# Opening of a transformer block on one core: the order of two accumulators' products, of one tile's squaring, and of the second half's transposes

## The chip, the cores and the metric

The kernel runs on one core of a Trainium2 chip. The metric is the device time of one execution in microseconds. Three executions of the kernel before took 1181.06, 1181.30 and 1181.48 us; the median is 1181.3.

The core has five engines with one instruction queue each. TensorE (PE in the profile, with its weight loads listed apart as PEld) multiplies matrices into PSUM, VectorE (DVE) and ScalarE (ACT) do elementwise work, GpSimd (POOL) does small elementwise work here, and SyncE (SP) issues most of the loads. Each queue is worked through in order; engines wait for one another by semaphores.

## The reference

One layer of a hybrid encoder: an RMSNorm with adaptive scale and shift, a combined projection, two head groups side by side (a state-space group and a chunked attention group), an output projection, a gated feed-forward part with a short convolution, and a final RMSNorm. Sequence 1024, width 1024, float32. Cut to what the change touches:

```python
c_act = jax.nn.silu(c)
mod = (c_act @ w_ada[l] + b_ada[l])[:, None, :]
sh_m, sc_m, g_m, sh_f, sc_f, g_f = jnp.split(mod, 6, axis=-1)
h = rmsnorm(x, norm_mix_w[l]) * (1 + sc_m) + sh_m
z, xbc, dt_raw, q, k, v = jnp.split(h @ w_in[l], IN_SPLITS, axis=-1)
y_ssd = ssd_mixer(z, xbc, dt_raw, ...)
y_att = chunk_attention(q, k, v, rel_bias[l])
x = x + g_m * (jnp.concatenate([y_ssd, y_att], axis=-1) @ w_out[l])
h = rmsnorm(x, norm_ffn_w[l]) * (1 + sc_f) + sh_f
x = x + g_f * conv_ffn(h, w_up[l], ffn_conv_w[l], w_down[l])
return rmsnorm(x, final_norm_w)
```

The opening of the kernel computes h, and from it q and k of the first two head pairs and v of the same pairs.

## The kernel before

**Numbers in two parts.** Every float32 operand of a large product is split into a high part and a low part (float32r), and a product is three matmuls, high x high, high x low and low x high (`mm3`, lines 83 to 86). Splitting costs one conversion for the high part and one subtraction for the low part (`split`, lines 88 to 94).

**Tiles of the opening.** The 1024 tokens are eight x tiles of 128 tokens (`xts`, tiles 0 to 7); tiles 0 to 3 are the first half (hh = 0), tiles 4 to 7 the second (hh = 1). The 1024 features are eight feature blocks of 128 (kt = 0 to 7). An x tile is loaded (`x_load`, L324), squared and summed along its features (`x_square`: ScalarE's Square with an accumulator, L287, and a small step that adds epsilon, L331; or one VectorE reduction, L333), turned into a reciprocal root on GpSimd (`x_rstd`, L339) and scaled in place (`x_scale`, L345 on ScalarE, L347 on VectorE). The tables `XL`, `XS` and `XM` (L37 to L39) say for tiles 4 to 7 at which feature block of the first half each is loaded, squared and scaled.

**An h block** (`h_block`, L295 to L307) is one feature block of one half, transposed: four TensorE transposes of 128x128, one for each x tile, into a PSUM bank (`tp`; there are two such banks), then the adaptive scale and shift, which also splits. In the first half ScalarE makes the high part (hH, L303) and a float32 copy (hf, L304); in the second ScalarE makes hf alone and VectorE casts it to hH (L306). VectorE's subtraction makes the low part (hL, L307). There are two hf buffers.

**What is multiplied.** For each half there are four accumulators of 128x512 (`accs`, acc in the profile: q and k of pair 0, q and k of pair 1) and two banks for v (`vps`, 128x256 twice in each). A feature block adds 12 matmuls of 128x512 (`first_qk`) and 12 of 128x256 (`first_v`). For each feature block of the first half the kernel also reduces two rows of w_ada on VectorE (`mod_col`, L146) to the scale and shift (amix, L435; bmix, L212), loads the weights (L440) and splits them: wsh on ScalarE (L442), wsl on VectorE (L444).

**Evacuation.** v's banks go out through ScalarE and VectorE (`evac_v`, L413). A q or k accumulator goes out as a high part by ScalarE (L243, L250) and a low part by VectorE (L244, L253), followed by transfers between partitions on SP's queue (L238). The first half's fourth accumulator is copied whole to `k1` by ScalarE (L485), because its place is still taken by an x tile, and is split at the end of the second half.

**What sets the order.** The program is written as one stream; a scheduler that simulates time puts each engine's instructions in order, and each engine then works strictly through its queue. Where `T.on` (or `V.on`, `A.on`) is true, instructions of that engine keep the order in which they are written; `tc.issue_after(i)` forces an instruction behind another. In the first half, feature blocks 0 to 5 are multiplied as they come, and blocks 6 and 7 are the tail, in written order: v's products of both blocks, v's evacuation, then each accumulator's products of both blocks and its evacuation, with the second half's h blocks 0 and 1 behind the second accumulator. In the second half, blocks 0 to 3 are multiplied as they come and blocks 4 to 7 are the tail, an accumulator at a time; h blocks 2 to 7 are written one in each step kt = 2 to 7.

The opening starts the kernel and ends near 97 us, where attention has begun. Nothing behind it is changed.

Of the kernel before, what the change touches and what calls it, by code (L numbers as in the profile page):

```python
# [10 lines left out]
F32 = mybir.dt.float32  # L11
# [5 lines left out]
P = 128  # L17
D = 1024
S = 1024
KT = D // P  # L20
NT = S // P
# [12 lines left out]
GP = {1: {0: ((2, 0, BOTH), (2, 1, BOTH)), 2: ((2, 2, BOTH),)},  # L34
      2: {0: ((3, 0, BOTH), (3, 1, H0)), 2: ((3, 2, H0),)},
      3: {0: ((3, 1, H1),), 1: ((3, 2, H1),)}}
XL = (3, 5, 7, 7)  # L37
XS = (4, 6, 7, 7)
XM = (7, 7, 7, 7)  # L39
WARM = (8, 22)  # L40
KH = NF // 2

# [30 lines left out]
def tile_block(ctx: ExitStack, tc: tile.TileContext, x, ccol, pk, w_ada, w_first, w_ft, w_z,  # L73
# [221 lines left out]
    def h_block(hh, kt, js=(0, 1, 2, 3), tps=None):  # L295
        tps = h_tp(hh, kt) if tps is None else tps
        tmp = s0.tile([P, 512], F32, tag="hf", bufs=2, name="hf")
        b = slice(js[0], js[-1] + 1)
        hi, lo = (t[:, b] for t in ht(hh, kt))
        tps, tmp = c4(tps)[:, b], c4(tmp)[:, b]  # L300
        ab = dict(scale=amix[:, kt:kt + 1], bias=bmix[:, kt:kt + 1])
        if hh == 0:
            A.activation(hi, tps, AF.Identity, **ab)  # L303
        i = A.activation(tmp, tps, AF.Identity, **ab)  # L304
        if hh:
            V.tensor_copy(hi, tmp)  # L306
        return i, V.tensor_tensor(lo, tmp, f32(hi), ALU.subtract)  # L307
# [9 lines left out]
    xts = []  # L317
# [7 lines left out]

    def x_square(st, eng):
        ms = stat()
        junk = s0.tile([P, D], F32, tag="junk", name="junk") if eng is A else xts[NT - 2]
        if eng is A:
            norm_to(xts[st], junk, ms)  # L330
            A.activation(ms, ms, AF.Identity, bias=mhalf[:, 7:8])  # L331
        else:
            V.tensor_tensor_reduce(out=junk, in0=xts[st], in1=xts[st], scale=1.0 / D, scalar=EPS,  # L333
                                   op0=ALU.mult, op1=ALU.add, accum_out=ms)
        return ms

    def x_rstd(ms):
        r = stat()
        G.tensor_tensor(r, ms, mhalf[:, 0:1], ALU.pow)  # L339
        return r  # L340
# [25 lines left out]
    for j in range(2):  # L366
        k = slice(4 * j, 4 * j + 4)
# [23 lines left out]
    def first_qk(acc, n, hh, kts, js=slice(0, 4)):  # L391
        w = slice(n * P, (n + 1) * P)
        for kt in kts:
            mm3(c4(acc)[:, js], wsh[:, kt, w], ws_lo(kt)[:, w], *(t[:, js] for t in ht(hh, kt)),
                kt == 0 and js.start == 0, kt == KT - 1, hh == 0)
# [19 lines left out]
    xr = {}  # L415
    for hh in range(2):
        accs = [(ps0, ps0b)[n // 2].tile([P, 512], F32, tag="acc0", bufs=2, name="acc0") for n in range(4)]
        vps = [psv.tile([P, 2, 256], F32, tag=t, bufs=1, name="vps") for t in ("acc", "pv")]
        split_at = KT - (2, 4)[hh]
        evj = []  # L420

        def ev_half():
            if not evj:
                t = s0.tile([P, D], F32R, tag="junk", name="evl")
                evj.extend((t[:, 512:1024], t[:, 0:512]))
            return evj.pop()

        evs.append(ev_half)
        tail = range(split_at, KT)
        for kt in range(KT):  # L430
            if hh == 0:
                at = last_lo.ins if kt == 1 else bm.ins if kt else None
                mod_col(SC_M + kt, wu.tile([P, 1024], F32, tag="wh", name="adat"), at)
                mod_col(SH_M + kt, adw[:, kt % 2, :], at)
                V.scalar_tensor_tensor(amix[:, kt:kt + 1], modc[:, SC_M + kt:SC_M + kt + 1],  # L435
                                       pkt[:, NMIX + kt:NMIX + kt + 1], am1[:, kt:kt + 1],
                                       op0=ALU.mult, op1=ALU.add)
                bm = mod_shift(bmix, SH_M, kt)
                t = raw_tile(768)
                nc.sync.dma_start(t, w_first[kt])  # L440
                with tc.issue_after(bm.ins) if not kt else ExitStack():
                    (A.activation(wsh[:, kt, :], t, AF.Copy) if kt else V.tensor_copy(wsh[:, kt, :], t))  # L442
                with tc.issue_after(bm.ins):
                    V.tensor_tensor(ws_lo(kt), t, f32(wsh[:, kt, :]), ALU.subtract)  # L444
                for st in range(4, NT):
                    if XL[st - 4] == kt:
                        V.tensor_copy(xts[st][:, 0:1], amix[:, min(kt, 6):min(kt, 6) + 1])
                        x_load(st)
            if hh == 0 or kt > 1:
                hb = i, last_lo = h_block(hh, kt, tps=None if hh or not kt else tps)  # L450
            if hh == 0 and kt == 0:
                x_scale(3, r3, A, rest)
                V.on = A.on = T.on = False
            if hh == 0 and kt < KT - 1:
                tps = h_tp(0, kt + 1)
            if hh == 0:
                for st in range(4, NT):
                    if XS[st - 4] == kt:
                        with tc.issue_after(i.ins):
                            xr[st] = x_rstd(x_square(st, A))  # L460
                    if XM[st - 4] == kt:
                        e = A if st < 6 else V
                        with tc.issue_after((i if e is A else last_lo).ins):
                            x_scale(st, xr[st], e)
            if hh == 1 and kt == 3:
                wpin = hb
            if kt < split_at:
                for n in range(4):
                    first_qk(accs[n], n, hh, (kt,))
                first_v(vps, hh, (kt,))  # L470
        T.on, T.last = True, None
        if hh == 0:
            first_v(vps, 0, tail)
            evac_v(vps, 0)
            for n in range(4):
                first_qk(accs[n], n, 0, tail)
                if n == 1:
                    for kt in range(2):
                        T.on = False
                        h_block(1, kt)  # L480
                        T.on = True
                if n < 3:
                    evac_qkv(n // 2, n % 2, 0, accs[n], None, None)
            k1 = s0.tile([P, 512], F32, name="k1")
            A.activation(k1, accs[3], AF.Copy)  # L485
        else:
            for n in range(4):
                first_qk(accs[n], n, 1, tail)
                if n == 3:
                    es_0a.close()  # L490
                    ps1 = es_p1.enter_context(tc.tile_pool(name="ps1", bufs=1, space=PSUM,
                                                           reuse_waits="tile"))
                    s00 = scores(0, 0)
                    first_v(vps, 1, tail)
                evac_qkv(n // 2, n % 2, 1, accs[n], None, None)
            evac_v(vps, 1)
            evac_qkv(1, 1, 0, k1, None, None)
        T.on = False
# [1263 lines left out]
```

## Time and profile before

| | |
|---|---|
| median of three runs (lowest to highest) | 1181.3 us (1181.06 to 1181.48) |
| the profiled execution | 1181.23 us, of which the span from first to last instruction is 1179.5 us |
| granted TensorE clock, mean | 0.993 |
| TensorE busy from 0 to 24 us | 18.70 us |
| TensorE busy from 24 to 97 us | 70.95 of 73.00 us |
| TensorE busy from 97 us to the end | 1064.15 of 1082.5 us |

Rows of the timeline give the start in us from the span's start, the length in us, the engine, the line, the operation and its tiles as out<-in, the partitions and elements, and how many like instructions are merged (xN); in brackets stands the idle time before it and the instruction that ended it. Rows of waits give the total in us, how often, and the longest. Rows by stage give the stretch, its length, the busy time and the number of instructions of an engine, then the granted TensorE clock (1.00 is full), the share of the DMA engines' time and GB/s. A matmul's end is modelled: consecutive starts tell the pace better than lengths. Tile names are without buffer numbers: tp is a transposed block's bank, qk an x tile or, later, a q or k tile in the same place, wsh and wsl the weights' parts, raws and adat buffers of loads.

### The profile page before, as it was taken

The numbers are of one execution on the slowest core, as the hardware profiler recorded it, in microseconds if no ns is written. First come the engines' busy times: TensorE is split into PE (matmuls) and PEld (weight loads), VectorE is DVE, ScalarE is ACT, GpSimd is POOL, SyncE is SP. The second block draws the span as 40 slices with busy tenths as digits, with TensorE's granted clock in tenths as the row PEclk, the third lists the DMA queues.
The fourth block names the chain that finished last, engine by engine and source line by source line (L and its number), as shares of the span: only waits on it lengthen the run. The fifth ranks groups of instructions, "written<-read, shape, count | busy, mean of one in ns | idle before, by whom it ended". The sixth has DMA issues, their size and how long they took to land.

```text
span 1179.5 us, 15776 instructions
## 1 busy us (share of the span) xinstructions
PE 1153.8 (98%) x5831; PEld 975.9 (83%) x5831; DVE 906.5 (77%) x1350; ACT 586.8 (50%) x981; POOL 155.8 (13%) x179
## 2 busy tenths in 40 slices
PE   8999999999999999999999999999999999999996
PEld 7878888788889888887788888888888888888885
DVE  6736455588895678558999988898888869666986
ACT  5726555664345575487444453434433445433454
POOL 2003333340000165200000000000000000000622
PEclk8999999999999999999999999999999999999998
DMA  8735323155577532141233222332233378633444
GB/s 327 275 97 142 82 81 85 39 179 174 185 254 284 193 112 87 63 152 36 90 116 134 94 82 96 131 124 73 98 107 116 117 271 300 249 118 124 161 134 152
DMA packets 63741, 169.15 MB, mean 143 GB/s; under 512 B 6880, under 2 KB 7344, under 8 KB 62256
## 3 DMA queue, kind: packets, MB, share of 16 engines
q1 hardware_dynamic: 56320, 143.11, 36.6%
q10 hardware_dynamic: 7344, 25.04, 5.4%
q8 instruction: 46, 0.75, 0.3%
q14 instruction: 31, 0.25, 0.1%
HBM read 125.87 MB, written 32.81 MB: 135 GB/s over the span
## 4 chain that ended last, share of the span: by engine, by line
PE 78%; DVE 11%; ACT 4%; issue 3%; DMA 3%; POOL 1%; SPq 0%; POOLq 0%; ACTq 0%; DVEq 0%
PE wops L874 6%; PE dn L86 5%; PE dn L85 5%; PE dn L84 5%; PE uY L86 5%; PE uY L85 5%; PE uY L84 5%; PE uX L86 3%; PE uZ L86 3%; PE uZ L85 3%; PE uZ L84 3%; PE uX L85 3%; PE uX L84 3%; PE acc L84 3%; PE acc L85 2%
## 5 line engine op out<-in xcount | busy, mean ns | idle before, releaser
L84 PE MATMUL dn<-w 128*128 128x512 f32 x296 | 107.4, 389 | 0.0
L85 PE MATMUL dn<-w 128*128 128x512 f32 x296 | 107.3, 389 | 0.0
L86 PE MATMUL dn<-w 128*128 128x512 f32 x296 | 99.8, 390 | 0.1
L86 PE MATMUL uY<-tH,w 128*128 128x512 f32 x248 | 96.5, 389 | 0.0
L84 PE MATMUL uY<-tH,w 128*128 128x512 f32 x248 | 96.5, 389 | 0.0
L85 PE MATMUL uY<-tL,w 128*128 128x512 f32 x248 | 96.5, 389 | 0.0
L1623 POOL TENSOR_TENSOR ya<-ya,xs 128x512 f32<-128x512 f32 x4 | 18.2, 4588 | 551.0 <-ACT xs L1619 551.0
L93 ACT ACTIVATE w<-ya 128x1024 fp32r<-128x1024 f32 (+1 forms) x41 | 39.1, 954 | 85.3 <-PE uY L86 75.2
L874 PE MATMUL wops<-hH,yhl 128*128 128x512 f32 x224 | 73.0, 398 | 0.7 <-DVE yhl L94 0.6
L86 PEld LDWEIGHTS dn<-w 128*128 128x128 f32 x296 | 55.4, 188 | 12.2 <-DVE w L94 0.8
L84 PEld LDWEIGHTS dn<-w 128*128 128x128 f32 x296 | 55.6, 188 | 11.6
L85 PEld LDWEIGHTS dn<-w 128*128 128x128 f32 x296 | 55.6, 188 | 11.4
L548 POOL TENSOR_SCALAR p<-p,st 128x640 f32<-128x640 f32 (+4 forms) x64 | 44.2, 699 | 115.0 <-DVE st L547 111.2
L93 ACT ACTIVATE w<-xs 128x1024 fp32r<-128x1024 f32 (+1 forms) x41 | 39.1, 954 | 36.9 <-PE uY L86 31.1
L542 DVE CUSTOM_DVE_ANT_0 p<-s,bias 128x640 f32<-128x640 f32 (+4 forms) x58 | 38.0, 674 | 23.1 <-PE tp L577 9.6
L94 DVE TENSOR_TENSOR pt<-tp,pt 128x512 fp32r<-128x512 f32 (+2 forms) x72 | 41.6, 595 | 17.3 <-ACT pt L93 16.9
L85 PEld LDWEIGHTS uY<-tL,w 128*128 128x128 f32 x248 | 46.6, 188 | 9.7
L84 PEld LDWEIGHTS uY<-tH,w 128*128 128x128 f32 x248 | 46.6, 188 | 9.7
L86 PEld LDWEIGHTS uY<-tH,w 128*128 128x128 f32 x248 | 46.6, 188 | 9.6
L1297 DVE SCALAR_TENSOR_TENSOR a<-cv,pkt,a 128x1023 f32<-128x1023 f32 (+1 forms) x40 | 51.0, 1276 | 0.1
L84 PE MATMUL s<-hH,wh 128*128 128x512 f32 x128 | 50.6, 395 | 0.1
L86 PE MATMUL s<-hH,wl 128*128 128x512 f32 x128 | 50.3, 393 | 0.0
(503 smaller groups left out, 3387.1 us busy)
## 6 DMA issues: line engine op xcount, KB each, us to landing
xs<-in_w_ada_dram SPq DMA_DIRECT2D x20, 512.0 KB, 4.6
gz<-a ACTq DMA_DIRECT2D x10, 1024.0 KB, 5.1
ya<-in_w_up_dram SPq DMA_DIRECT2D x11, 768.0 KB, 4.2
xs<-in_w_up_dram SPq DMA_DIRECT2D x11, 768.0 KB, 4.2
adat<-in_w_ada_dram SPq DMA_DIRECT2D x16, 512.0 KB, 5.9
raws<-in_w_ft_dram SPq DMA_DIRECT2D x15, 512.0 KB, 4.1
qk<-qk SPq DMA_DIRECT2D x56, 128.0 KB, 2.3
wos<-in_w_ada_dram SPq DMA_DIRECT2D x12, 512.0 KB, 4.6
```

What stands on the lines that cost most here:

```text
L84: T.matmul(ps, lh, rh, start=start, stop=False, skip_group_check=more)
L85: T.matmul(ps, lh, rl, start=False, stop=False, skip_group_check=more)
L86: T.matmul(ps, ll, rh, start=False, stop=stop, skip_group_check=more)
L93: i = A.activation(hi, src, AF.Copy) if ehi is A else ehi.tensor_copy(hi, src)
L94: return i, elo.tensor_tensor(lo, src, f32(hi), ALU.subtract)
L542: V.tensor_tensor_reduce(out=dst, in0=src, in1=bsl, scale=-1.0, scalar=3e38, op0=ALU.add, op1=ALU.min, accum_out=nm)
L548: last_g.append(G.tensor_scalar(pv_, pv_, rr, 1.0, op0=ALU.mult, op1=ALU.mult).ins)
L874: i = op(*a, **k)
L1297: V.scalar_tensor_tensor(a[:, j:S], c[:, 0:S - j], w[2 - j], a[:, j:S], op0=ALU.mult, op1=ALU.add)
L1623: G.tensor_tensor(src, src, fnr[:, halves[1]], ALU.mult)
```

## The change

Four things move; no arithmetic is added or removed.

1. Tile 5 is loaded at feature block 4 instead of 5 (`XL`), and tile 4 is scaled at block 6 instead of 7 (`XM`).
2. Tile 7 is squared by VectorE instead of ScalarE, into a buffer of the pool `wu`.
3. In the first half's tail the first two accumulators' products of block 6 are put between v's products of block 6 and v's products of block 7.
4. In the second half the h blocks 2 to 7 are written two with each of the steps kt = 0, 1, 2, instead of one with each of kt = 2 to 7.

```diff
-XL = (3, 5, 7, 7)
+XL = (3, 4, 7, 7)
 XS = (4, 6, 7, 7)
-XM = (7, 7, 7, 7)
+XM = (6, 7, 7, 7)
...
     def x_square(st, eng):
         ms = stat()
-        junk = s0.tile([P, D], F32, tag="junk", name="junk") if eng is A else xts[NT - 2]
+        junk = (s0.tile([P, D], F32, tag="junk", name="junk") if eng is A else xts[NT - 2] if st < 4
+                else wu.tile([P, 1024], F32, tag="wh", name="xjunk"))
...
-            if hh == 0 or kt > 1:
-                hb = i, last_lo = h_block(hh, kt, tps=None if hh or not kt else tps)
+            if hh == 0:
+                i, last_lo = h_block(0, kt, tps=tps if kt else None)
+            elif kt < 3:
+                for k in (2 * kt + 2, 2 * kt + 3):
+                    hb = h_block(1, k)
+                    if k == 3:
+                        wpin = hb
...
-                        with tc.issue_after(i.ins):
-                            xr[st] = x_rstd(x_square(st, A))
+                        with tc.issue_after((last_lo if st == 7 else i).ins):
+                            xr[st] = x_rstd(x_square(st, V if st == 7 else A))
...
-            if hh == 1 and kt == 3:
-                wpin = hb
...
         if hh == 0:
-            first_v(vps, 0, tail)
+            first_v(vps, 0, tail[:1])
+            for n in range(2):
+                first_qk(accs[n], n, 0, tail[:1])
+            first_v(vps, 0, tail[1:])
             evac_v(vps, 0)
             for n in range(4):
-                first_qk(accs[n], n, 0, tail)
+                first_qk(accs[n], n, 0, tail[1:] if n < 2 else tail)
```

What this makes of the queues, at the three places of which the prediction speaks. The numbers behind names tell buffers apart; behind the opening the engines' orders are the same as before.

TensorE, second half, before: the last v products of block 3 (vps), the four last h blocks' transposes, and the start of the tail.

```order
L66 MATMUL vps<-wsh,hL_87 128x256
L292 MATMUL tp_752<-ident,qk 128x128 x4
L292 MATMUL tp_761<-ident,qk 128x128 x4
L292 MATMUL tp_770<-ident,qk 128x128 x4
L66 MATMUL acc_632<-hH_85,wsh 128x512
L292 MATMUL tp_779<-ident,qk 128x128 x4
L66 MATMUL acc_632<-hL_87,wsh 128x512
```

TensorE, second half, now: block 1, where h blocks 4 and 5 are transposed, and the first rows of block 2 with h blocks 6 and 7.

```order
L84 MATMUL acc_634<-hH_85,wsh 128x512
L292 MATMUL tp_679<-ident,qk 128x128 x4
L85 MATMUL acc_631<-hL_87,wsh 128x512
L292 MATMUL tp_688<-ident,qk 128x128 x4
L86 MATMUL acc_631<-hH_85,wsl 128x512
...
L84 MATMUL acc_631<-hH_85,wsh 128x512
L292 MATMUL tp_721<-ident,qk 128x128 x4
L292 MATMUL tp_730<-ident,qk 128x128 x4
L85 MATMUL acc_631<-hL_87,wsh 128x512
```

The sixteen transposes stood together between block 3 and the tail; now they stand among the products of blocks 1 and 2.

TensorE at the seam between the halves, before (acc_213 is the first half's fourth accumulator, tp_587 and tp_596 the second half's h blocks 0 and 1, tp_686 its block 2).

```order
L66 MATMUL acc_213<-hH_84,wsl_121 128x512
L292 MATMUL tp_587<-ident,qk 128x128
L292 MATMUL tp_596<-ident,qk 128x128
L292 MATMUL tp_686<-ident,qk 128x128 x4
L84 MATMUL acc_632<-hH_85,wsh 128x512
```

The same place now.

```order
L66 MATMUL acc_213<-hH_84,wsl_121 128x512
L292 MATMUL tp_586<-ident,qk 128x128 x2
L292 MATMUL tp_595<-ident,qk 128x128 x2
L292 MATMUL tp_637<-ident,qk 128x128 x4
L84 MATMUL acc_631<-hH_85,wsh 128x512
```

Two tiles' transposes, not one, now stand behind the first half's last product. Further on, the second half's fourth accumulator (acc_634) starts only behind the transposes of h block 3.

ScalarE, first half, blocks 6 and 7, before, from block 6's hf to the first evacuation of v.

```order
L304 ACTIVATE hf<-tp_459,bmix,amix 128x512
L442 ACTIVATE wsh<-raws 128x768
L303 ACTIVATE hH_84<-tp_502,bmix,amix 128x4x128
L304 ACTIVATE hf<-tp_502,bmix,amix 128x512
L345 ACTIVATE qk<-qk,st_72 128x1024
L287 ACTIVATE junk,st_72<-qk 128x1024
L331 ACTIVATE st_72<-st_72,mhalf 128x1
```

ScalarE now: from the same hf, and, at the seam, the copies of the accumulators between the hf of the second half.

```order
L304 ACTIVATE hf<-tp_459,bmix,amix 128x512
L346 ACTIVATE qk<-qk,st_72 128x1024
L287 ACTIVATE junk,st_72<-qk 128x1024
L332 ACTIVATE st_72<-st_72,mhalf 128x1
L443 ACTIVATE wsh<-raws 128x768
L303 ACTIVATE hH_84<-tp_502,bmix,amix 128x4x128
...
L492 ACTIVATE k_629<-acc_213 128x512
L304 ACTIVATE hf<-tp_586,bmix,amix 128x512
L243 ACTIVATE qk<-acc_212 128x512
L304 ACTIVATE hf<-tp_595,bmix,amix 128x512
```

Tile 4's scale and tile 5's square moved ahead of block 7's weight conversion, and the third accumulator's copy, which stood ahead of the fourth's, moved behind the first hf.

## The prediction

> **What bounds the kernel now.** I read first the page's head, for what the whole span hangs on.
>
> ```profile
> span 1179.5 us, 15776 instructions
> PE 1153.8 (98%) x5831; PEld 975.9 (83%) x5831; DVE 906.5 (77%) x1350; ACT 586.8 (50%) x981; POOL 155.8 (13%) x179
> ```
>
> TensorE has work in 98% of the span, so a change that adds and removes no arithmetic can only win back places where TensorE stands or crawls. Second I asked who made TensorE wait from 24 us, where the opening's steps have become regular, to 97 us, where the opening ends.
>
> ```profile
> PE tp L292 <- ACT hf L304: 1.6, 2, 1.1
> ```
>
> The largest row has only 1.6 us, all of it ahead of the second half's transposes. But a matmul's end is modelled, so waiting inside a run of short instructions can count as busy. Third, therefore, the same stretch by stage, TensorE alone (stretch, length, busy with the number of instructions, clock, DMA share, GB/s):
>
> ```profile
> 47.53:50.40 2.87, 2.87 (x26) 1.00 0.70 247
> 50.40:56.59 6.19, 6.19 (x32) 1.00 0.07 17
> 56.59:58.57 1.98, 0.84 (x8) 1.00 0.52 114
> ...
> 75.86:82.65 6.79, 5.88 (x30) 1.00 0.00 0
> 82.65:90.84 8.19, 8.19 (x38) 1.00 0.52 114
> ```
>
> The last row is the undisturbed pace: from 82.65 to 90.84 lie 36 products of 128x512 (the counts also hold instructions that cross an edge), 8.19 / 36 = 0.2275 us each. The row above it starts at the four last transposed blocks and holds 16 transposes and 12 such products. The products are worth 12 x 0.2275 = 2.73 us, so the transposes and their waits took 6.79 - 2.73 = 4.06 us. That is the place that matters; the second is 56.59 to 58.57, where TensorE had eight instructions to do in 1.98 us. The clock is 1.00 in all rows and plays no part.
>
> **The late blocks (the last part of the change).** What the 4.06 us consist of, in the timeline (start, length, engine, line; in brackets the idle time before and who ended it):
>
> ```profile
> 39.65 0.60 PE L292 MATMUL tp<-ident,qk 128*128 128x128 f32 x4
> 40.01 0.48 PE L85 MATMUL acc<-hL,wsh 128*128 128x512 f32 x1
> 40.33 0.39 PE L86 MATMUL acc<-hH,wsl 128*128 128x512 f32 x1
> ...
> 75.86 1.04 PE L292 MATMUL tp<-ident,qk 128*128 128x128 f32 x8
> 77.37 0.66 PE L292 MATMUL tp<-ident,qk 128*128 128x128 f32 x4 [0.48 <-ACT hf L304]
> ```
>
> At 75.86 two blocks fill both transpose banks; the third waits for ScalarE to empty one, and the products behind it wait for VectorE's casts of the blocks just made. At 39.65, in the first half, a block's four transposes stand among products with nothing to wait for: 40.01 - 39.65 = 0.36 us, and the product behind them is followed after 0.32 instead of 0.23, so 0.45 a block. The change puts two blocks with the second half's feature block 1, one product apart (2 x 0.45), and two back to back with feature block 2 (8 x 0.09 + 0.09 = 0.81): together 1.71 us. Gain: 4.06 - 1.71 = **2.35 us**. Bounds: at the bare 0.36 a block it is 2.62; at the pace of the eight at 75.86 (77.37 - 0.48 - 75.86 = 1.03, so 0.51 a block) it is 2.0. I take 2.35, because the new places look like the one at 39.65.
>
> The Trainium skill, "TensorE: Matmul & The Clock Gate", section "Back-to-back issue gap", gives about 81 ns per 128-column matmul in a stream with its weight loads. By that the sixteen would cost 1.3 us and the time would be an estimated 1178.3; the trace has 90 ns in the same kind of place, and its figure is the one used.
>
> The new places must not wait in their turn. TensorE's queue is strict here, so a bank that is not yet empty would hold all products behind it. What ScalarE and VectorE have to do ahead of the new blocks, and where the second half's feature blocks 1 and 2 start now:
>
> ```profile
> 61.44 2.00 ACT L93 ACTIVATE wh<-raws 128x1024 fp32r<-128x1024 f32 x2
> ...
> 62.65 2.35 DVE L94 TENSOR_TENSOR wl<-raws,wh 128x1024 fp32r<-128x1024 f32 x2
> ...
> 63.31 0.86 PE L84 MATMUL acc<-hH,wsh 128*128 128x512 f32 x3
> 67.50 0.40 PE L84 MATMUL acc<-hH,wsh 128*128 128x512 f32 x1
> ```
>
> With 0.2 us won at the first gap (below), block 1 starts near 63.1 and the two new blocks are transposed after its fourth and fifth product, near 64.0 and 64.7. ScalarE read the banks that they need before its two conversions, by 61.5. It is through with those at some 63.6 and, at 0.72 a hf, empties both banks by 66. Block 2 starts at 67.5 + 0.9 - 0.2 = 68.2 and transposes after its first product, at 68.4: over 2 us spare. VectorE, 2.35 us behind its own conversions, has cast the last block by some 72; its products come after 77. So nothing waits.
>
> **The first gap.** Its chain, TensorE, ScalarE and VectorE:
>
> ```profile
> 56.59 0.38 PE L292 MATMUL tp<-ident,qk 128*128 128x128 f32 x2
> 58.11 0.66 PE L292 MATMUL tp<-ident,qk 128*128 128x128 f32 x4 [1.14 <-ACT hf L304]
> 58.57 1.20 PE L84 MATMUL acc<-hH,wsh 128*128 128x512 f32 x4
> ...
> 56.79 0.60 ACT L485 ACTIVATE k<-acc 128x512 f32<-128x512 f32 x1 [0.87 <-PE acc L66]
> 57.28 1.44 ACT L304 ACTIVATE hf<-tp,bmix,amix 128x512 f32<-128x512 f32 x2
> ...
> 58.09 0.43 DVE L306 CAST hH<-hf 128x512 fp32r<-128x512 f32 x1 [0.41 <-ACT hf L304]
> ```
>
> The first half's last product is over when the transposes start at 56.59. ScalarE then copies that accumulator out (56.79), makes hf (57.28), VectorE casts it (58.09), the second half's first product starts at 58.57: 1.98 us. In the new order the copy of the last accumulator still stands ahead of the first hf, and the last transposes (tiles 6 and 7, four now) still come after the last product, so the 1.98 us stay. Four of the eight transposes, not two, now lie inside them for nothing. Before, six transposes in three places made 50.40 to 56.59 last 6.19 - 24 x 0.2275 = 0.73 us longer than its 24 products, 0.24 a pair; one pair less in front gives up to 0.24 us. I take **0.2 us**. The other end: the third accumulator's copy now comes between the first two hf, and VectorE's half of it behind the first cast (58.0 + 0.6 + 0.69, about 59.2). The second half's fourth accumulator, placed behind the next transposes, starts near 60 and does not meet it; if the third needed that bank, it would wait 59.2 - 58.9 = 0.3 us. So between -0.3 and +0.24.
>
> **Accumulators ahead of v's last block, tile 7 on VectorE, tile 5 earlier.** These reorder equal work; each costs nothing while this cover lasts:
>
> ```profile
> 30.00:40.00 10.00, 10.00 (x65) 8.96 (x64) 9.36 (x21) 6.51 (x12) 0.00 (x0) 1.00 1.02 392
> ...
> 43.42 0.85 ACT L442 ACTIVATE wsh<-raws 128x768 fp32r<-128x768 f32 x1
> 47.50 1.15 ACT L345 ACTIVATE qk<-qk,st 128x1024 f32<-128x1024 f32 x1
> 49.92 1.04 ACT L287 ACTIVATE junk<-qk 128x1024 f32<-128x1024 f32 x1
> ...
> 42.89 1.22 DVE L146 CUSTOM_DVE_ANT_0 adat<-adat,rows 128x1024 f32<-128x1024 f32 x1
> 47.64 0.69 DVE L307 TENSOR_TENSOR hL<-hf,hH 128x512 fp32r<-128x512 f32 x1 [0.70 <-ACT hf L304]
> 51.57 0.69 DVE L94 TENSOR_TENSOR v<-vps,v 128x512 fp32r<-128x512 f32 x1 [3.23 <-ACT v L93]
> ```
>
> Tile 4's scale and tile 5's square (with its small steps 49.92 - 47.50 = 2.42 us) move ahead of feature block 7's weight conversion, from 43.42 to 45.84; its h block, until now over at 48.33 (the 47.64 row), ends about 0.5 later, near 48.8. Tile 5's load now goes in front of feature block 7's three loads: 512 KB at 392 GB/s is 1.34 us. VectorE's two reductions of that block stand one place later (42.89 becomes about 44.05), which takes up most of it; at worst another 0.8. The cover: v's feature block 7 used to start after a quarter of v's 2.87 us, at 48.25. Now v's block 6 (half of the 2.87) and six products (1.37) run first, so it starts at 47.53 + 1.44 + 1.37 = 50.3, 1.5 us after 48.8 and 0.7 after the worst case. VectorE's new square is an instruction of the same form as the one at 42.89, 1.22 us; it falls into the 3.23 us that VectorE idles before 51.57. ScalarE loses a square of 1.04. Sum 0; without the cover, up to 0.5.
>
> **Sum.** 0.2 + 2.35 = 2.55 us. The profiled execution took 1181.23 (span 1179.5 and 1.7 around it), 0.07 under the median of the three runs, less than their spread of 0.42. 1181.23 - 2.55 = **1178.7 us**. It arrives at the end if the later stages start from TensorE's progress. The one long stretch whose chain leaves TensorE begins so:
>
> ```profile
> 318.32 0.24 PE s L85
> 318.59 1.07 ACT wh L93
> ```
>
> A product frees the buffer, ScalarE follows, then VectorE and loads; that stretch moves with TensorE.
>
> **Rivals.** (1) *Part of it is lost*: the third accumulator's bank holds up a product (-0.3 instead of +0.2) and transposes cost 0.51 (2.0), so 1.7 us; or later stages, started earlier, wait longer for their own loads. For it: the evacuation does move back. Against: the order puts the fourth accumulator behind transposes. About 1179.6 to 1180.2. (2) *Slower*: one mechanism, ScalarE's strict queue at tile 5. If tile 5 or block 7's loads arrive late, the square holds the weight conversion, block 7's h block and v's products. It decides once the h block is later than 50.3, 1.5 us beyond my reckoning; to be slower than before by 0.2% (2.4 us) the delay must be 1.5 + 2.55 + 2.4 = 6.4 us. At 3 us beyond that point the time would be 1181.7, at 5 us 1183.7. Against: tile 5 is asked for earlier than before. (3) *The gain is larger*: the transposes disappear fully under weight loads and the first gap shrinks by a further half, 2.62 + 1.2 = 3.8, so 1177.4. Against: the copy still leads the chain. (4) *It doesn't do what it says*: the blocks would still clump; the printed order rules that out, so it has no chance of its own.
>
> **How the numbers follow.** Forecast 0.74, own range 1178.2 to 1179.2 (2.0 to 3.0 us); part lost 0.14; larger 0.05; slower 0.07. What a measurement here can tell from no change is about 0.2%, 2.4 us, so the line is at 1178.9. Of the forecast's 0.74 I put 0.58 under that line, since the terms' middle lies 0.2 below it, and 0.16 above. Faster: 0.58 + 0.05 = 0.63; same: 0.16 + 0.14 = 0.30; slower: 0.07. Range: from 1177.6, between forecast and larger gain, to 1180.6, beyond the partial loss.
>
> **What would show it.** Right: TensorE's transposes from 63 to 70 us with no idle time before them, none at 75; the second half's last product near 88.3 instead of 90.8; the gap of 1.98 us still there, about 0.2 earlier. Wrong: a wait for ScalarE's hf before the transposes near 68, for VectorE before v's block 7 near 50, or a later stage whose start has not moved.

## The result and the profile after

| | before | changed |
|---|---|---|
| median of 10 runs (lowest to highest) | 1180.14 us (1179.0 to 1181.48) | 1176.88 us (1173.8 to 1179.83) |
| ratio of the two, 95% interval | | 0.9972 [0.9961, 0.9984] |
| the profiled execution | 1181.23 us | 1178.57 us |
| its granted TensorE clock, mean | 0.993 | 0.993 |

The change makes the kernel faster by 0.28%, 3.3 us. The forecast of 1178.7 us had the direction and was 1.8 us too high; the measured time lies below the low end of its range, 1177.6. Between the two profiled executions the difference is 1181.23 - 1178.57 = 2.66 us, close to the sum of 2.55. So there are two questions: whether the terms stand where the sum put them, and why the runs differ by more than the profiled pair.

The head of the changed kernel's page:

```profile
span 1176.8 us, 15778 instructions
PE 1153.2 (98%) x5831; PEld 976.3 (83%) x5831; DVE 907.7 (77%) x1352; ACT 585.9 (50%) x978; POOL 156.0 (13%) x179
```

The work is the same as before (TensorE busy 1153.2 against 1153.8 us); what went is time in which TensorE stood. Its waits from 24 to 97 us in the changed kernel, all of them (total, how often, the longest):

```profile
PE tp L292 <- ACT hf L304: 0.9, 1, 0.9
```

The same stretches by stage as before the change (stretch, its length, then busy time and number of instructions of TensorE, its weight loads, VectorE, ScalarE and GpSimd, clock, DMA share, GB/s):

```profile
60.40:75.86 15.46, 15.46 (x94) 13.58 (x92) 9.41 (x15) 6.66 (x9) 0.00 (x0) 1.00 0.38 108
75.86:82.65 6.79, 6.79 (x38) 5.83 (x37) 0.69 (x1) 0.60 (x1) 0.00 (x0) 1.00 0.02 5
```

The stretch from 75.86 to 82.65, in which the sixteen transposes and 12 products stood, is now full of products. The timeline of the changed kernel shows where the transposes went, and the seam between the halves:

```profile
56.79 0.60 PE L292 MATMUL tp<-ident,qk 128*128 128x128 f32 x4
58.31 0.66 PE L292 MATMUL tp<-ident,qk 128*128 128x128 f32 x4 [0.92 <-ACT hf L304]
58.77 0.95 PE L84 MATMUL acc<-hH,wsh 128*128 128x512 f32 x3
...
64.42 0.60 PE L292 MATMUL tp<-ident,qk 128*128 128x128 f32 x4
65.10 0.60 PE L292 MATMUL tp<-ident,qk 128*128 128x128 f32 x4
68.82 1.04 PE L292 MATMUL tp<-ident,qk 128*128 128x128 f32 x8
```

The late blocks' transposes stand at 64.42, 65.10 and 68.82 with no idle time before them. The gap from the last transposes' start to the second half's first product is 58.77 - 56.79 = 1.98 us, as before.

To see where TensorE gains, its instructions of two traces are laid beside each other, counted back from the last, and their starts subtracted. This table, worked out from the traces, gives at some moments of the profile before how many us later (+) or earlier (-) TensorE is than there; the moments are such that the same kind of instruction stands there in both orders:

| moment in the profile before, us | 47.5 | 48.6 | 58.5 | 61.0 | 82.7 | 318 | 386.7 | 395 | 1169 |
|---|---|---|---|---|---|---|---|---|---|
| changed | +0.42 | +0.41 | +0.20 | +0.20 | -2.10 | -2.10 | -2.54 | -2.54 | -2.67 |

Across the seam, from 47.5 to 58.5, the changed kernel wins 0.22 us, put at 0.2; from 61.0 to 82.7 it wins 2.30, the late blocks, put at 2.35. The second half's last product starts at 88.49 us, 2.12 earlier than before (90.61). Then nothing is lost up to 318 us, and 0.44 is won near 386. It comes to 47.5 late by 0.42. The reason is in the clock.

**The clock.** Three stretches of the profile before (columns as above):

```profile
15.50:24.00 8.50, 7.40 (x28) 6.08 (x29) 6.06 (x13) 5.58 (x8) 0.29 (x2) 0.60 0.90 318
24.00:47.50 23.50, 23.50 (x145) 20.91 (x144) 22.26 (x48) 13.93 (x20) 0.82 (x1) 1.00 1.01 377
...
380.00:392.00 12.00, 9.63 (x65) 9.23 (x65) 5.17 (x19) 2.02 (x5) 0.00 (x0) 0.86 0.32 102
```

Just behind 15.5 us, and again behind a wait of TensorE near 384 us, the granted clock is below 1. The trace's clock record says more: it falls to 0.5 for 6.83 us in the opening, for 3.41 us near 387 us, and for the last 6.9 us, behind TensorE's last product; and twice 3.41 is 6.83. In the changed kernel's profile the opening's half clock has the same length but starts and ends 0.95 us later. At 20 us the two are level to 0.01 us; then the changed kernel's products go on at half clock for 0.95 us longer, which is the +0.42. The opening's products at half clock are paid in both, so the two profiled executions compare well. But the pieces of 3.41 us are not the same in every run, as the experiments show.

### The profile page after: what moved, and what is told of

It reads as the page before. It is cut to its first block, busy times and chain, and to the rows that moved or that the text cites. A ratio compares the mean times of both kernels' runs of the same rounds, so it can differ in the third digit from the quotient of the medians.

```text
span 1176.8 us, 15778 instructions
## 1 busy us (share of the span) xinstructions
PE 1153.2 (98%) x5831; PEld 976.3 (83%) x5831; DVE 907.7 (77%) x1352; ACT 585.9 (50%) x978; POOL 156.0 (13%) x179
## 4 chain that ended last, share of the span: by engine, by line
PE 82%; DVE 10%; ACT 3%; issue 2%; DMA 2%; POOL 1%; SPq 0%; POOLq 0%; DVEq 0%; ACTq 0%
PE wops L881 6%; PE dn L86 5%; PE dn L85 5%; PE dn L84 5%; PE uY L86 5%; PE uY L84 5%; PE uY L85 5%; PE uX L86 3%; PE uZ L86 3%; PE uZ L84 3%; PE uZ L85 3%; PE uX L84 3%; PE uX L85 3%; PE acc L84 3%; PE acc L85 3%; PE acc L86 3%
```

## The experiments

Each run below gives the median of its runs, beside runs of the kernel before on the same chip. Over all of them there are 81 runs of the kernel before with their mean clocks (mean time 1180.12 us), and with the ten of the result 21 of the changed kernel (1176.83).

**The changed kernel again**, with no edit.

> The changed kernel once more, beside the kernel before on the same chip. Theory A: the change itself is worth 2 to 2.7 us (ratio 0.9977 to 0.9983), all of it in the opening; the scatter of the changed kernel's ten times comes from TensorE's granted clock, which is 0.993 in some executions (near 1178.7 us) and 0.996 in others (near 1175 us), and the kernel before has the same two kinds of executions (near 1181.3 and 1177.8 us). Theory B: the change makes the kind with 0.996 likelier, so the kernel before stays at 0.993 to 0.994 and the ratio is 0.996 to 0.997 on the mean.

Measured: 1176.75 us (1175.08 to 1178.38, 11 runs), ratio 0.9976 [0.9967, 0.9985]. Mean times by the mean clock of the run:

| mean clock of the run | before | changed | difference |
|---|---|---|---|
| up to 0.993 | 1181.08 (36 runs) | 1178.36 (9) | 2.72 |
| 0.994 | 1180.11 (11) | 1177.20 (1) | |
| 0.995 and above | 1179.11 (34) | 1175.54 (11) | 3.57 |

One piece of 3.41 us at half clock is 3.41 / 2 / 1180 = 0.0014 of the mean, so the first and the last row are about two such pieces apart. The sorting is rough, though: in each of the 14 profiles of this document the clock is also half for the last 4.3 to 7.4 us, where TensorE has no work left, and that costs nothing but moves the mean by up to 0.0013, as much as one piece. Both kernels have either kind about equally often (44% and 43% of the runs in the first row), so the change does not bring the fuller clock.

The profile before is of the first row. The clocks of the three runs that were shown are not on record, but their times (1181.06 to 1181.48) lie at its mean; if such runs come 36 times in 81, three out of three have a chance of 0.09. By the table the change is worth 2.72 us in that row and 3.57 where the clock is fuller, as if something in it counted only then. But the runs of this experiment alone, beside the kernel before on the same chip, give 3.03 (1180.94 to 1177.91) and 2.85 (1178.97 to 1176.12), so the times do not show that.

**The late blocks alone**, the kernel before with part 4 and nothing else.

```diff
-            if hh == 0 or kt > 1:
-                hb = i, last_lo = h_block(hh, kt, tps=None if hh or not kt else tps)
+            if hh == 0:
+                i, last_lo = h_block(0, kt, tps=tps if kt else None)
+            elif kt < 3:
+                for k in (2 * kt + 2, 2 * kt + 3):
+                    hb = h_block(1, k)
+                    if k == 3:
+                        wpin = hb
```

> The kernel before with the last part of the change alone (two h blocks with each of the second half's first three feature blocks). Theory A: this part carries the gain: 2.2 us of the span (2.0 to 2.6), the gap at the seam stays 1.98 us as before. Rival: the three other parts carry half or more, and this one gives 1.2 us or less.

Measured: 1176.38 us (1175.64 to 1178.95, 11 runs), ratio 0.9976 [0.9967, 0.9986]. **Without the late blocks**, the changed kernel with that piece undone:

> The changed kernel without its last part. Theory A: 0 to 0.3 us faster than before in executions of like clock, the sixteen transposes stand together again and cost about 4 us with their waits. Rival: half the gain or more stays (over 1.2 us).

Measured: 1179.45 us (1177.27 to 1180.79, 11 runs), ratio 0.9991 [0.9983, 1.0000]. TensorE against the profile before, in us as above; both of these profiles have only one piece of 3.41 us at half clock in the opening:

| moment, us | 47.5 | 48.3 | 48.6 | 61.0 | 82.7 | 318 | 386.7 | 395 |
|---|---|---|---|---|---|---|---|---|
| late blocks alone | -1.15 | -1.15 | -0.37 | -0.35 | -2.61 | -2.68 | -3.20 | -4.71 |
| without late blocks | -0.99 | -0.99 | -1.00 | -1.21 | -1.19 | -1.26 | -1.54 | -1.53 |

The late blocks win 2.26 us between 61.0 and 82.7 in the one and nothing there in the other: the term holds.

In time the two runs don't add up as neatly: parts 1 to 3 alone win 0.7 us (1180.18 to 1179.45), but part 4 alone, 1176.38 us, is as fast as the changed kernel on the same chip, 1176.75. Part 4's runs had the fuller clock more often (8 of 11, against 6 of 11). Sorted as above, their mean is 1176.43 us at 0.995 and above, the changed kernel's 1176.12 beside them, and 1178.54 (2 runs) against 1177.91 (4) at 0.993 or less. So medians over mixed runs don't settle what parts 1 to 3 are worth.

The new thing stands between 48.3 and 48.6. Both kernels come there a good 1 us earlier than the profile before, since the opening crawled for 3.41 us less. The one without parts 1 to 3 loses 0.78 of it at one spot. The product that waits, first in the profile before and then here with its neighbours:

```profile
48.49 0.29 PE L66 MATMUL vps<-wsh,hL 128*128 128x256 f32 x1
...
47.21 0.28 PE L66 MATMUL vps<-wsl,hH 128*128 128x256 f32 x1
47.28 0.69 DVE L307 TENSOR_TENSOR hL<-hf,hH 128x512 fp32r<-128x512 f32 x1 [0.71 <-ACT hf L304]
48.03 0.39 PE L66 MATMUL vps<-wsh,hL 128*128 128x256 f32 x1 [0.54 <-DVE hL L307]
```

TensorE is in v's products of feature block 7 here and waits for VectorE's low part of that h block, which is over at 47.28 + 0.69 = 47.97. In the profile before, VectorE was through at 48.33, 0.16 us ahead of the product that reads it (48.49), so no wait showed. In the changed kernel:

```profile
48.54 0.69 DVE L307 TENSOR_TENSOR hL<-hf,hH 128x512 fp32r<-128x512 f32 x1 [0.69 <-ACT hf L304]
...
50.55 0.39 PE L66 MATMUL acc<-hH,wsl 128*128 128x512 f32 x1
...
50.81 0.36 PE L66 MATMUL vps<-wsh,hH 128*128 128x256 f32 x1
...
51.16 0.36 PE L66 MATMUL vps<-wsh,hL 128*128 128x256 f32 x1
```

The low part is there at 49.23; v's block 7 starts at 50.81, behind six products of the accumulators, and the product that reads the low part at 51.16: the margin of 0.16 us has become 1.9.

**A fuller clock in the opening.** Dummy products of the identity, 13 of them into a bank that nothing reads, keep TensorE working between the transposes of the first h block. First in the changed kernel:

```diff
             T.transpose(tps[:, j * P:(j + 1) * P], xts[4 * hh + j][:, kt * P:(kt + 1) * P], ident)
+            if T.on and hh == kt == 0 and j:
+                warm_up((0, 8, 3, 2)[j])
```

> The changed kernel with 13 dummy matmuls of the identity (results unused) put into the waits between the first h block's transposes, at 12 to 17 us of the span. If the half clock from about 16 to 23 us follows from TensorE's waits there, it is gone or shorter in all executions: granted clock 0.996 or more, times near 1175 us, spread under 2 us. If it does not depend on those waits, the same two groups of times and clocks appear as in the changed kernel, and the dummies cost 0 to 0.5 us.

Measured: 1178.46 us (1174.21 to 1180.34, 11 runs), ratio 0.9984 [0.9973, 0.9996]. The half clock is gone from the opening here and in the three filled profiles below, so it did follow from TensorE's waits there, and TensorE leads by 3.87 us at 318. But 1.2 of it are lost at 384, and the expected times near 1175 us with a spread under 2 did not come. Then the same dummies in the kernel before, in the kernel with part 4 alone, and in that with parts 3 and 4 (part 3's lines as in the change's diff):

> The kernel before, with the 13 dummy products that keep TensorE's clock up in the opening. Theory T (a wait in the first half's tail): in the order before, v's products of block 7 need VectorE's low part of h block 7, and in the profile before TensorE needed it only 0.16 us after it was there (48.33 and 48.49 us). With the fuller clock TensorE arrives there 1.3 to 1.5 us earlier and waits about 1 us for it, so that at 60 us it leads the profile before by only 0.2 to 0.5 us. Rival R (no such wait; what is lost is lost elsewhere): no wait before v's block 7, and the lead at 60 us is 1.3 us or more.

> The kernel before with the second half's transposes moved (part 4 alone) and the same dummy products. Theory T: the same wait of about 1 us for VectorE's low part before v's block 7, and a lead of 2.5 to 2.9 us over the profile before at 97 us (2.35 from the blocks, the rest as in the filled kernel before). Rival R: lead 3.7 us or more at 97 us. In time, under T about 2.3 us less than the filled kernel before.

> Parts 3 and 4 (accumulators' products ahead of v's block 7, and the transposes), without the tiles' loads, scales and squares moved, and the same dummy products. Theory T with part 3 as the cover: no wait before v's block 7, lead at 97 us 3.5 to 3.9 us, as in the filled changed kernel (3.87), so about 1 us more than with part 4 alone. Rival P (the moved tile steps, parts 1 and 2, are what counts): the wait is still there or has moved to the seam, and the lead at 97 us is 2.5 to 2.9 us. If the restart near 384 us is held by its own chain, as it was in the filled changed kernel, of the lead beyond some 2.6 us nothing arrives at the end.

Measured: 1182.44 us, 1180.35 us and 1183.03 us (11 runs each), ratios 1.0017 [1.0009, 1.0026], 0.9998 [0.9989, 1.0007] and 1.0018 [1.0008, 1.0028]. TensorE against the profile before:

| moment, us | 47.5 | 48.6 | 58.6 | 61.0 | 97 | 318 | 386.7 | 395 |
|---|---|---|---|---|---|---|---|---|
| before, filled | -1.49 | +0.15 | -0.02 | -0.01 | -0.04 | -0.04 | +1.93 | +1.94 |
| part 4, filled | -1.68 | -0.04 | -0.22 | -0.22 | -2.51 | -2.60 | +0.19 | -0.41 |
| parts 3 and 4, filled | -1.43 | -1.36 | +0.74 | +2.13 | -0.20 | -0.27 | +1.18 | +1.95 |
| changed, filled | -1.44 | -1.39 | -1.59 | -1.59 | -3.87 | -3.87 | -2.64 | -2.63 |

In the order before, 1.64 us of lead vanish between 47.5 and 48.6, in both kernels that have it. (At 61.0 nothing is left of the filled kernel before's lead, where 0.2 to 0.5 us were expected.) Most of it is one wait, here in the one with part 4:

```profile
48.36 0.38 PE L66 MATMUL vps<-wsh,hL 128*128 128x256 f32 x1 [0.89 <-DVE hL L309]
```

So the wait for VectorE's low part is there in the order before as soon as TensorE comes earlier, and at 97 us the changed kernel leads the one with part 4 alone by 3.87 - 2.51 = 1.36 us. Between the two filled kernels in the old order, part 4 is worth 1182.44 - 1180.35 = 2.09 us in time. With part 3 but without parts 1 and 2 the wait at 48.6 is gone and a larger one stands at the seam:

```profile
57.46 0.44 PE L292 MATMUL tp<-ident,qk 128*128 128x128 f32 x2 [1.76 <-DVE qk L349]
```

The second half's first transposes wait 1.76 us for VectorE's scaling of an x tile, and the clock record has 3.41 us of half clock right behind, which makes the loss at 61.0 larger. This refutes the expectation that part 3 is the cover by itself: part 3 takes the wait away, and the changed kernel, which has parts 1 and 2 as well, does not have the one at the seam; so these have the tiles ready in time. Which of the two does it was not tried.

Not expected at all: the filled kernels lose near 384 us. The filled kernel before is level with the unfilled one at 318 (-0.04) and 1.93 late at the restart, so the times of filled and unfilled kernels can't be compared. What of it the dummies cause is open: behind the opening every engine's order is the same, but by 330 us, with TensorE still where it was, VectorE has fallen 0.6 to 1.0 us behind it in the filled kernels. There it waits for a load of w_ada rows: 0.57 us in the profile before, 1.54 in the filled kernel before, though the load is issued at the same time (325.90 and 325.87). The place itself could be settled.

**The restart near 384 us.** In the profile before, SP's longest wait there (total, how often, the longest), then its queue, VectorE, ScalarE and TensorE (SPq rows are issues of DMAs):

```profile
SPq L755 <- DMA wsl<-wos: 9.2, 3, 4.4
...
375.93 1.37 SPq L782 DMA_DIRECT2D wsl<-wos  x1
379.29 0.81 SPq L755 DMA_DIRECT2D wos<-in_w_out_dram  x2
380.20 0.85 SPq L799 DMA_DIRECT2D raws<-in_w_z_dram  x2
...
377.11 1.42 DVE L91 SCALAR_TENSOR_TENSOR wzl<-raws,wzh 128x520 fp32r<-128x520 f32 x2 [3.75 <-ACT wzh L90]
...
385.98 1.28 ACT L90 ACTIVATE wzh<-raws 128x520 fp32r<-128x520 f32 x2 [5.36 <-DMA raws<-in_w_z_dram]
...
386.67 0.51 PE L84 MATMUL zps<-wzh,hH 128*128 128x260 f32 x2 [2.37 <-ACT wzh L90]
```

Read from the end: TensorE waits for ScalarE's conversion of z weights, that one for their load. VectorE had read the last of the two buffers that the load fills at 377.11 + 1.42 = 378.53. The load was issued at 380.20: it stands on SP's queue behind two loads of w_out, and those wait for a store of the buffer that they overwrite (the first row). The edit puts the w_out loads behind the z loads; it was made in the changed kernel, in the changed kernel with the next edit, and in the kernel before.

```diff
-            nc.sync.dma_start(t, w_z[ch, :, a * 520:(a + 1) * 520])
+            zload = nc.sync.dma_start(t, w_z[ch, :, a * 520:(a + 1) * 520])
...
+        ws.append(zload.ins)
         return ws
...
     wz = wz_weights(0)
-    wout_get(2, 3)
+    with tc.issue_after(wz[4]):
+        wout_get(2, 3)
```

> The changed kernel, with the last two loads of the z weights put on SP's queue ahead of the four loads of w_out that stand before them and wait for a store. Theory L (the restart near 384 us hangs on SP's queue, not on TensorE): the buffers of the z weights are free at 376.9 us (VectorE's 375.43 and two of 0.71), the loads were issued at 378.85; issued at once, they end 1.5 to 2 us earlier, TensorE's wait of 1.5 us goes to 0 or nearly, and the window of half clock behind it (1.7 us lost) goes with it in most runs: 1.5 to 3.2 us less than the changed kernel, about 1173.6 to 1175.3. Rival E (TensorE's own progress or the conversions set the restart): the wait stays within 0.5 us and the time within 1176.3 to 1177.3. A loss is possible if the moved loads of w_out are late for their splits.

> The kernel before with the z loads first, and nothing else. Theory L: the wait of 2.4 us near 384 us falls to 0.5 or less, 2 to 3.5 us less than before. Against the changed kernel with the z loads first it shows what the change is worth when nothing behind the opening waits: the sum of the prediction with no loss and no gain behind the opening says 2.55 us; if the tail's wait for VectorE counts in the runs with a fuller clock, it is 2.6 to 3.3 us on the mean over runs.

Measured: the changed kernel 1173.82 us (1173.25 to 1174.96, 5 runs), the kernel before 1176.74 us (1176.48 to 1177.47, 8 runs); ratios to the kernel before 0.9948 [0.9934, 0.9961] and 0.9971 [0.9961, 0.9981]. The changed kernel with the z loads first:

```profile
375.27 1.05 SPq L806 DMA_DIRECT2D raws<-in_w_z_dram  x2
376.38 1.84 SPq L762 DMA_DIRECT2D wos<-in_w_out_dram  x4
```

Its stretch by stage:

```profile
380.00:392.00 12.00, 12.00 (x103) 12.00 (x102) 9.47 (x27) 5.52 (x14) 0.00 (x0) 1.00 0.32 98
```

TensorE no longer waits there (12.00 of 12.00 busy, in the profile before 9.63), and the piece of half clock behind the wait is gone (clock 1.00, before 0.86). By the expectations, this is the theory that the restart hangs on SP's queue. With the edit the scheduler also reorders instructions of TensorE, VectorE and ScalarE between 381 and 406 us, alike in both kernels, so the win is that of the edit as a whole. The kernel before wins 1180.68 - 1176.74 = 3.9 us by it, beside the runs of its chip; the changed kernel 1176.75 - 1173.82 = 2.9, with the first number from another chip, where the kernel before took 1180.18.

The kernel before, which spread from 1178.09 to 1181.36 in 12 runs on this chip, now spreads over 1.0 us although its runs' clocks go from 0.994 to 0.997; those at 0.996 and 0.997 took 1176.69 and 1176.78 us, like the others. So most of what set its runs apart was this restart. That a fuller clock in the opening no longer shows in its time fits the wait at 48 us, which would take it; its one profile has two pieces of half clock there and doesn't show it. The last run adds part 4 alone to this:

> The kernel before with part 4 alone and the z loads first: beside the two kernels with the z loads first (the kernel before 1176.74 us, the changed kernel 1173.82) it gives the late blocks alone and, by difference, parts 1 to 3. Theory T (parts 1 to 3 free TensorE from a wait for VectorE that stands only when the opening's clock is fuller): the times lie close together, as the kernel before's did (1176.48 to 1177.47), 2.4 us below them at 1174.3 to 1174.5, so that parts 1 to 3 are worth 0.2 to 1.0 us; a trace with one window of half clock or none in the opening shows TensorE waiting for VectorE ahead of v's block 7, and one with two shows no such wait. Rival: parts 1 to 3 are worth nothing, and the median is 1173.6 to 1174.0.

Measured: 1174.46 us (1174.13 to 1174.75, 5 runs), ratio 0.9945 [0.9931, 0.9958]; on another chip, where the kernel before had 1180.84 against 1180.68. With the z loads first the late blocks are thus worth 1176.74 - 1174.46 = 2.28 us and parts 1 to 3 a further 1174.46 - 1173.82 = 0.64 (by the means of the runs 2.41 and 0.47; the second is not apart from its scatter, since the changed kernel's five runs reach from 1173.25 to 1174.96). Of that, 0.2 is the seam, which the profiles with parts 1 to 3 win and this one does not; it was in the prediction's sum. So 0.27 to 0.44 us are left for the wait. Its profile has two pieces of half clock in the opening, and TensorE is 0.28 us earlier at 47.5 than in the profile before: even that is lost (+0.06 at 48.6), against the expectation of no wait with two pieces.

**The copy at the seam.** The prediction said that the copy of the first half's fourth accumulator leads the chain across the gap of 1.98 us. The edit puts it behind the second half's first two hf on ScalarE.

```diff
-                        h_block(1, kt)
+                        hb = h_block(1, kt)
...
-            A.activation(k1, accs[3], AF.Copy)
+            with tc.issue_after(hb[0].ins):
+                A.activation(k1, accs[3], AF.Copy)
```

> The changed kernel with the copy of the first half's fourth accumulator put behind the second half's first two hf on ScalarE. The prediction said that this copy leads the chain across the gap of 1.98 us. Theory C (the copy is the chain): the first hf starts 0.3 to 0.5 us earlier and the gap from the last product's end to the second half's first product falls from 1.98 to 1.5 to 1.7 us. Rival D (the last transposes, which also come after the last product, hold hf just as long): the gap falls by 0.15 us or less. In both the second half's fourth accumulator may wait longer for its bank.

> The same as the run with the z loads first, and the copy of the first half's fourth accumulator behind the two hf. The one look showed the gap between the halves 0.27 us shorter with that. Expected: 0.27 us earlier than the run with the z loads first at 60 us, and, since the wait near 384 us no longer takes it, 0.2 to 0.3 us less in time (less than the interval of one comparison).

Without the z loads first there is one execution, 1177.35 us. Its timeline:

```profile
55.30 0.60 PE L292 MATMUL tp<-ident,qk 128*128 128x128 f32 x4
56.55 0.66 PE L292 MATMUL tp<-ident,qk 128*128 128x128 f32 x4 [0.65 <-ACT hf L304]
57.01 0.73 PE L84 MATMUL acc<-hH,wsh 128*128 128x512 f32 x2
```

The gap is 57.01 - 55.30 = 1.71 us, 0.27 less: between the two expectations (at most 1.7 if the copy is the chain, 1.83 or more if the last transposes hold hf as long). Taken off, the copy gives 0.27 of the 0.49 us by which it led; then the transposes are next. With the z loads first the profile has the expected 0.27 us again (0.48 won between 48.6 and 58.5 us, against 0.21 without the copy moved), and it is the fastest version tried: 1173.35 us (1172.57 to 1174.56, 5 runs), ratio to the kernel before 0.9945 [0.9933, 0.9958]. Its distance to the same without the copy moved, 0.47, lies within the scatter of either.

## Why the prediction was right in its main term and wrong in its time

**Late blocks: right.** Put at 2.35 us, 2.25 to 2.31 between 61.0 and 82.7 us in all ten profiles that have them, whatever the clock, and 2.28 in time with the z loads first. The transposes stand where they were said to: from 63 to 70 us without idle time, none at 75. So the four blocks cost 4.06 less these 2.25 to 2.31, 1.75 to 1.81 us, where the sum had 1.71 at 0.45 or less a block. By the 81 ns per matmul that the Trainium skill, "TensorE: Matmul & The Clock Gate", section "Back-to-back issue gap", gives, the gain would be an estimated 2.76 us; every profile lies below that.

**The seam: right.** The gap of 1.98 us stayed in the profiled pair, and 0.22 was won there for 0.2; the other profiles with parts 1 to 3 have 0.20 to 0.22, or 0.50 with the copy moved.

**Parts 1 to 3 at nothing: the term that was mis-sized.** The cover that the prediction named is what the traces show: h block 7 ends 50.81 - 49.23 = 1.6 us ahead of v's block 7, put at 1.5. But it reckoned only whether the new order would wait, and not what the old one would pay if TensorE came earlier. One of the rows it quoted held half of that: VectorE's low part ended at 47.64 + 0.69 = 48.33, and in the same profile the product that reads it started 0.16 us later. Where TensorE comes 0.28 us earlier or more, the old order loses time there (0.34 to 1.64 us in four profiles) and the new one does not. In time that is 0.27 to 0.44 us beyond the seam's 0.2 with the z loads first, not apart from scatter; the traces show the mechanism more surely than the times show its worth.

**The base: the step that failed.** The text took the profiled execution as the kernel's time, "0.07 under the median of the three runs, less than their spread of 0.42". But the profile was an execution at a mean clock of 0.993, and the three runs lie where such runs do, which was in part bad luck of the draw; over 81 runs the mean is 1180.12, 1.11 us less. With "the clock is 1.00 in all rows and plays no part" it looked at the rows of the changed stretch only; on the same page the clock row has 8 tenths in its first slice. The miss is 1178.68 - 1176.83 = 1.85 us on the means: 1.11 from the base and 3.29 - 2.55 = 0.74 from the gain. With the z loads first the gain is 2.92, so the term put at nothing accounts for up to half of the 0.74.

**Later stages move with TensorE: true to 367 us, not at 384.** The row at 318 us was read rightly, but a second wait, hidden behind the head's 98%, hangs on SP's queue and not on TensorE; its 2.4 us are TensorE's only wait between 360 and 420 us in the profile before. In the profiled pair it gave 0.4 back in the change's favour; in the filled changed kernel it took 1.2 of a lead of 3.87. This is the second mechanism of the first rival, and it took nothing from the change as measured. The third rival, a larger gain, came near the measured time, but not by its mechanism: the transposes did not vanish under weight loads, and the gap did not shrink. (Its 2.62 still charges 0.36 us a block; blocks that cost nothing would have given 4.06.)

What stays open: why the load near 330 us takes longer in the kernels with the dummies; and whether the 0.37 us between the gain over all runs (3.29) and that with the z loads first (2.92) is the restart or scatter.

## What to carry to other kernels

A sum made against one profiled execution needs to know which kind of execution that is: read the granted clock over the whole span, not only in the rows of the change, before taking three runs that agree for the kernel's time. For a reordering that seems to cost and win nothing, ask also how near the old order is to a wait; a margin of 0.16 us is one that other runs will cross. And a load that waits on a queue behind a load for another buffer is worth more than the change studied here: moving it won about 3 us in one kernel and 3.9 in the other.

## What the hardware showed that was not expected

TensorE's clock fell to one half for pieces of 3.41 us or twice that, behind waits of TensorE shorter than a piece: 2.37 us in the profile before and 1.50 in the changed kernel near 384 us, 1.76 and 0.76 close together at the seam with parts 3 and 4 alone. The same place did not always have it. With the late blocks alone:

```profile
15.50:24.00 8.50, 7.52 (x34) 6.43 (x35) 6.44 (x13) 5.35 (x8) 0.29 (x2) 0.80 0.94 337
...
380.00:392.00 12.00, 10.46 (x86) 10.06 (x85) 7.05 (x20) 4.89 (x10) 0.00 (x0) 1.00 0.20 65
```

Here the clock is 0.80 in the opening (0.60 in the profile before) and 1.00 near 384 us, though TensorE was idle there for 12.00 - 10.46 = 1.54 us as well. The Trainium skill, "TensorE: Matmul & The Clock Gate", section "Part 1: The HAM clock gate", has the clock decided by free-running windows of 3413 ns, at half or full rate; the lengths and the change from run to run agree with that. Its rule in the same part, no idle gaps above about 3.4 us, is too mild for this kernel: the measurement decides, and 1.5 us were enough in some runs.

The traces say more. In each of the 14, the changes of the clock lie whole multiples of 3.41 us apart, so the span can be cut into pieces of that length on its own grid, and TensorE's idle time counted in each. A piece at full clock with up to 1.44 us idle was always followed by one at full clock, one with 1.89 us or more always by one at half; from 1.50 to 1.74 us three went to half and four stayed. Inside the span a piece at half clock with 0.65 us idle or more was followed by another (eight of them), one with 0.41 or less by full clock. So what counts is how much of a wait falls into one piece, and the grid starts elsewhere in each execution: all 1.50 us of the changed kernel's wait near 384 lay in one piece, and 1.44 of the 1.54 with the late blocks alone. Idle time is from modelled ends, so the borders are rough.

The opening gives back part of what the half clock takes. In the filled kernel before TensorE is 2.6 us earlier than in the profile before at 24 us, but 1.4 at 28, and keeps that up to 47.5. In between, at 24.66 us of its own time, stands one wait for VectorE's low part, here as its row of waits:

```profile
PE acc L85 <- DVE hL L309: 0.8, 1, 0.8
```

VectorE is busy for 22.26 of the 23.50 us from 24 to 47.5 in the profile before, so it has little room to come earlier itself.
